# A gated decoder layer on one core: row sums turned on TensorE, and two tiles of h turned by DMA

## The chip, the cores and the metric

The kernel runs on one core of a Trainium2 chip. The metric is the device time of one execution in microseconds (us), taken as the median of repeated runs. A core has five instruction streams that run side by side and meet at semaphores: TensorE (PE in the profile, with PEld for its weight loads), VectorE (DVE), ScalarE (ACT), GpSimd (POOL) and SyncE (SP, which here only issues DMAs). Matrix products read from the on-chip memory SBUF and write to the accumulation memory PSUM; DMAs move data between SBUF and the device memory. Most DMAs are issued from SP's queue, a few from POOL's.

## The reference

One layer works on 1024 prompt tokens and 8 sample tokens, with a model width of 1024, all in 32-bit floats. What matters here:

```python
xn = _rmsnorm(h, pre_g)
proj = jnp.einsum('bld,de->ble', xn, w_in)          # 1024 -> 7 x 1024
u, v, z_a, x_b, z_b, g_a, g_b = jnp.split(proj, SPLITS, axis=-1)
vn = _layernorm(jax.nn.gelu(v), ln_g, ln_b)
y_a = u * _chunk_spatial_mix(vn, w_s, b_s) * jax.nn.silu(z_a)
...
m = (jax.nn.sigmoid(g_a) * jnp.einsum('ble,ed->bld', y_a, w_pa)
     + jax.nn.sigmoid(g_b) * jnp.einsum('ble,ed->bld', y_b, w_pb))
h = h + _rmsnorm(jnp.einsum('bld,de->ble', m, w_out), post_g)
e = jnp.einsum('blp,pd->bld', p, w_ple)
gate = jax.nn.sigmoid(jnp.einsum('bld,de->ble', _rmsnorm(h, ple_in_g), w_pg))
h = h + _rmsnorm(gate * e, ple_out_g)
```

Two places bear on the change. The spatial mix multiplies each chunk of 128 tokens by a lower-triangular 128x128 matrix per head, tril(W_s), and adds a bias b_s. Since vn = (v normalised) * ln_g + ln_b, the part with ln_b is the row sum of tril(W_s) times ln_b, one number per head and token. And the last product, with w_pg, needs h with the features along the partitions, while h is made with the tokens along them; so h has to be transposed.

## The kernel before

All large products are done with one level of Strassen's scheme (seven products P1 to P7 for a 2x2 block product) on operands that are split into a high and a low part, each product in three matmuls of reduced-precision format. A step of the stream is one such product: 12 matmuls of 512 columns, or 24 of 260. The stream runs over v, g_a, (u, z_a), (x_b, z_b and the pooling), g_b, w_pa, w_pb, then w_out and at last w_pg ("the gate product"), the last two by pairs of token tiles: pair i holds the tiles 2i and 2i+1 of 128 tokens each.

The order of instructions is not written out by hand beyond the opening. Every operation is handed to a planner (lines 56 to 300), which notes a due time for it, from its place in TensorE's stream and what depends on it, then plays all engines through with a duration for each kind of operation, and emits the instructions of each engine in the order that comes out. Work that is due later gives way to work that is due earlier; an instruction that has begun is not interrupted, and each engine runs its list in order. The first three steps are in a fixed order; from line 1733 on, the planner orders all of it. Tiles in SBUF come from a pool of 46 slots (line 31), and a slot is given to the next user when its last reader is done. The weights of a step are split three steps ahead (line 32).

The row sums. `ln_loads` (line 931) loads W_s as the tile ws and ln_g, ln_b as 16 rows of the tile lnvec. `spatial_weights` (line 943), put after the first step of g_a (line 1267), clears the upper triangles, sums the rows on VectorE into a tile of 128 tokens x 8 heads (rowsums), and stores it to device memory by a DMA that turns it on the way, so that the destination has 8 rows of 128. It also transposes the eight matrices on TensorE (bank psw) and lnvec into columns (bank lncol). `spatial_offsets` (line 963), eight steps later, reads the rows back, broadcast to all partitions (tile off), and makes of them the offsets that the users of z_a add.

The turning of h. For each tile t, `out_finish` (line 1405) scales h, adds the layer's input to it by an accumulating DMA from POOL's queue, and stores the result. `gate_norm` (line 1421) takes the sum of squares on ScalarE for the normalisation. `gate_input` (line 1438) transposes h in eight 128x128 blocks on TensorE into two PSUM banks (pht), which ScalarE copies into big, the operand of the gate product. They are hung on the steps of the following pair (lines 1564 to 1566): `out_finish` after its first step, `gate_norm` after its second, `gate_input` after its seventh. Tiles of h are handled in the order 1, 0, 3, 2 and so on; the gate product reads pair 0 first, and its splits of big are written to tiles named hw.

There is another way in the code already, under `if t in BY_DMA`, and the tuple BY_DMA (line 1416) is empty. It is the way that v is turned in `v_planes` and `v_join` (lines 866 and 875): ScalarE copies the upper and the lower 16-bit halves of the 32-bit words into two planes (for h in a new slot, also named hw), one transposing DMA on SP's queue turns both planes at once, and ScalarE joins the halves into big in two instructions.

Of the kernel before, what the change touches and what calls it, by code (L numbers as in the profile page):

```python
# [15 lines left out]
P = 128  # L16
D = 1024
NB = D // P
# [282 lines left out]
@with_exitstack  # L301
def tile_hybrid_step(ctx, tc, *args):
    hybrid_step(ctx, tc, *args)


def hybrid_step(
# [7 lines left out]
    nc = tc.nc  # L314
# [15 lines left out]
    def slot(name, shape=(P, T), dt=F32):  # L330
        n_name[0] += 1
        return plan.tile(spool.tile(list(shape), dt, tag="slot", name=f"{name}_{n_name[0]}", bufs=SLOTS,
                                    padded_shape=None), "slot")
# [5 lines left out]
    def bank(name):  # L339
        n_name[0] += 1  # L340
        return plan.tile(bankp.tile([P, 512], F32, tag="bank", name=f"{name}_{n_name[0]}"), "bank")
# [8 lines left out]
    def split(src, hi, lo):  # L350

        nc.scalar.activation(out=hi, in_=src, func=AF.Copy)
        nc.vector.tensor_tensor(out=lo, in0=src, in1=f32(hi), op=ALU.subtract)

    def dma(out, in_, by=None):
        (by or nc.sync).dma_start(out=out, in_=in_)
# [11 lines left out]
    ident = cpool.tile([P, P], F32, tag="ident", name="ident")  # L368
# [3 lines left out]
    nc = plan  # L372
# [16 lines left out]
    def root(part, n=P, r=None):  # L389

        t, r = sm("ms"), sm("rstd") if r is None else r
        nc.vector.tensor_scalar(out=t[:n], in0=part[:n], scalar1=EPS, scalar2=None, op0=ALU.add)
        nc.gpsimd.tensor_tensor(out=r[:n], in0=t[:n], in1=mhalf[:n], op=ALU.pow)
        return r
# [144 lines left out]
    class Features:  # L539

        new = staticmethod(lambda: region("acc"))
        sums = (P, 2, WIDE)
# [15 lines left out]
    class Tokens:  # L558
# [4 lines left out]
        sums = (P, 2, HALF)  # L563
# [359 lines left out]
    lnt = {}  # L923
# [7 lines left out]
    def ln_loads():  # L931
        lnt["ws"] = slot("ws", (P, NB, P))
        dma(lnt["ws"], w_s.rearrange("h t s -> t h s"))
        vec = lnt["vec"] = slot("lnvec", (P, P))
        for i, v in enumerate((ln_g, ln_b)):
            dma(vec[i * NB : (i + 1) * NB, :], v[0].rearrange("(k p) -> k p", p=P))

    def ln_rows():
        lnt["g"] = row_broadcast(ln_g[0], "lng")
# [3 lines left out]
    def spatial_weights():  # L943

        ws = lnt["ws"]
        nc.gpsimd.affine_select(out=ws, in_=ws, pattern=[[0, NB], [-1, P]], compare_op=ALU.is_ge,
                                fill=0.0, base=0, channel_multiplier=1)
        sums = cpool.tile([P, NB], F32, tag="rowsums", name="rowsums")
        nc.vector.tensor_reduce(out=sums, in_=ws, op=ALU.add, axis=mybir.AxisListType.X)
        dma(kept["rowsum"].rearrange("h t -> t h"), sums)  # L950
        lnt["wst"] = []
        for h4 in range(0, NB, 4):
            w = slot("wst", (P, 4, 2, P), F32R)
            ps = bank("psw")
            for i in range(4):
                nc.tensor.transpose(ps[:, i * P : (i + 1) * P], ws[:, h4 + i, :], ident)
            split(ps.rearrange("p (h t) -> p h t", t=P), w[:, :, 0], w[:, :, 1])
            lnt["wst"].append(w)
        ps = bank("lncol")
        nc.tensor.transpose(ps[:, : 2 * NB], lnt["vec"][: 2 * NB, :], ident[: 2 * NB, : 2 * NB])  # L960
        nc.vector.tensor_copy(lncol, ps[:, : 2 * NB].rearrange("p (i k) -> p i k", i=2))

    def spatial_offsets():

        off = lnt["off"] = slot("off", (P, NB, P))
        dma(off, kept["rowsum"].partition_broadcast(P))
        for h in range(NB):
            nc.vector.scalar_tensor_tensor(out=off[:, h], in0=off[:, h], scalar=lncol[:, 1, h : h + 1],
                                           in1=lnt["bs"][:, h * P : (h + 1) * P], op0=ALU.mult, op1=ALU.add)
# [31 lines left out]
    kept = {}  # L1001
# [262 lines left out]


    at(vsteps[2][3], ln_loads)
    at(gasteps[0][0], spatial_weights)
    for i, u in enumerate(vusers):

# [54 lines left out]
    p, l, c = gbsteps[2], gbsteps[3], pasteps[0]  # L1324
    turn_over(yaop, l, [*l[1:], c[0]])
    p, l, c = pasteps[2], pasteps[3], pbsteps[0]
# [86 lines left out]

    rin = lambda t: vsums[: rows(t), t, :1]

    BY_DMA = ()

    def words_of(t):
        return big.bitcast(U16)[:, :, 2 * t * P : 2 * (t + 1) * P]

    def gate_norm(t):
# [6 lines left out]
        root(n, r, rin(t))  # L1428
        if t not in BY_DMA:
            return  # L1430
# [7 lines left out]
    def gate_input(t):  # L1438
# [5 lines left out]
        for k4 in (slice(0, 4), slice(4, NB)):  # L1444
            if t in BY_DMA:
                nc.scalar.activation(out=words_of(t)[:, k4].rearrange("p k (t w) -> p k t w", w=2),
# [323 lines left out]
```

## Time and profile before

| what | value |
|---|---|
| median of three runs | 993.81 us (993.17 to 995.39) |
| the profiled execution | 993.5 us |
| its span, first to last instruction | 991.8 us |
| mean granted clock of TensorE | 0.998 |
| instructions | 15979 |
| moved by DMAs | 173.48 MB in 106154 packets, of which 25503 under 512 bytes |

In lines of the profile, an entry such as `big<-pht` names the tile that is written and the one that is read, without buffer numbers. L299 is a helper through which all planned operations pass, so tiles and engines, not lines, tell the operations apart. In the timeline the columns are start, length, engine, line, operation, `out<-in`, shapes and a count where several were merged; brackets give the idle time of the engine before it and what ended it. Lengths of matmuls contain their pipeline, so what one costs is seen from the starts of its neighbours. SPq and POOLq are the issuing of DMAs on those queues; the length is that of the issue, not of the transfer.

### The profile page before, as it was taken

The page shows a single profiled execution, that of the slowest core. Times are in us where ns is not written, and L with a number is a line of the kernel's source. Part 1 is how long each engine was busy: PE and PEld are TensorE (multiplying, and loading weights), DVE is VectorE, ACT ScalarE, POOL GpSimd, SP SyncE. Part 2 cuts the span into 40 slices and gives each one's busy share as a digit, 9 for nine tenths or more (in the row PEclk, how much of TensorE's full clock was granted, in tenths as well). Part 3 has the DMA queues.
Part 4 walks back from the last instruction along what each step waited for, and adds up shares of the span by engine and source line. Part 5 has one row for each costly group of instructions (what it writes and reads, how often), then busy time and mean ns, then how long its engine had stood idle before and what let it go on. Part 6 is the DMA issues. An engine that isn't in the chain of part 4 may idle for free. (4 is left out here: it accounts for less than half of the span.)

```text
span 991.8 us, 15979 instructions
## 1 busy us (share of the span) xinstructions
PE 977.3 (99%) x6102; PEld 877.1 (88%) x6102; DVE 797.6 (80%) x1238; ACT 523.4 (53%) x884; POOL 68.5 (7%) x142
## 2 busy tenths in 40 slices
PE   8999999999999999999999999999999999999996
PEld 7789989999998999999999999999999988888885
DVE  6796569787769888979897987697799898779596
ACT  7778987565434433344442333552353364677463
POOL 2100001000000000000000100000000001213111
PEclk9999999999999999999999999999999999999999
DMA  9335573322373353656735085973663543399546
GB/s 338 132 104 117 119 151 128 128 84 78 118 259 145 120 204 135 224 197 212 259 119 193 15 272 203 318 285 121 241 229 137 176 176 69 84 308 362 137 109 191
DMA packets 106154, 173.48 MB, mean 175 GB/s; under 512 B 25503, under 2 KB 64879, under 8 KB 106070
## 3 DMA queue, kind: packets, MB, share of 16 engines
q1 hardware_dynamic: 103982, 165.08, 49.0%
q0 software_dynamic: 2048, 7.37, 4.4%
q8 instruction: 48, 0.79, 0.3%
q14 instruction: 28, 0.23, 0.1%
q10 hardware_dynamic: 48, 0.01, 0.0%
HBM read 114.84 MB, written 53.87 MB: 170 GB/s over the span
## 5 line engine op out<-in xcount | busy, mean ns | idle before, releaser
L299 DVE TENSOR_TENSOR u<-acc,u 128x520 f32<-128x520 f32 (+1 forms) x90 | 62.7, 696 | 38.3 <-PE acc L299 35.0
L299 POOL TENSOR_TENSOR rstd<-ms,mhalf 128x1 f32<-128x1 f32 (+1 forms) x36 | 30.4, 848 | 192.5 <-DVE ms L299 191.5
L299 POOL MEMSET u<- 128x8 f32 x35 | 4.5, 164 | 502.6 <-PE acc L299 251.3
L299 ACT ACTIVATE u<-acc 128x512 f32<-128x512 f32 x39 | 23.3, 597 | 25.0 <-PE acc L299 24.6
L299 ACT ACTIVATE paw<-pas 128x512 fp32r<-128x512 f32 x16 | 10.1, 628 | 30.5 <-DVE pas L299 25.2
L299 ACT ACTIVATE pbw<-pbs 128x512 fp32r<-128x512 f32 x16 | 10.0, 629 | 28.0 <-DVE pbs L299 24.9
L299 DVE TENSOR_TENSOR big<-big 128x1024 f32<-128x1024 f32 (+4 forms) x20 | 23.6, 1219 | 0.0
L299 ACT ACTIVATE big<-mix 128x256 f32<-128x256 f32 x32 | 12.1, 383 | 18.1 <-PE mix L299 17.3
L299 ACT ACTIVATE big<-v 128x1024 uint16<-128x1024 uint16 x16 | 18.5, 1175 | 5.1 <-DMA v<-vw 5.1
L299 PE MATMUL accm<-qh,wpoolw 128*128 128x260 f32 (+1 forms) x96 | 20.9, 319 | 0.0
L299 ACT ACT_TABLE_LOAD x13 | 16.7, 1283 | 7.2 <-PE acc L299 6.3
L299 ACT ACTIVATE zbw<-zbs 128x512 fp32r<-128x512 f32 x16 | 10.1, 629 | 16.6 <-DVE zbs L299 11.6
L299 DVE TENSOR_TENSOR acc<-acc,u 128x512 f32<-128x512 f32 (+1 forms) x16 | 11.2, 701 | 8.7 <-PE acc L299 8.7
L299 DVE TENSOR_TENSOR v<-acc,u 128x520 f32<-128x520 f32 (+1 forms) x9 | 6.3, 697 | 14.3 <-PE acc L299 14.2
L299 ACT ACTIVATE gbw<-gbs 128x512 fp32r<-128x512 f32 x16 | 10.0, 626 | 14.6 <-DVE gbs L299 12.1
L299 ACT ACTIVATE zaw<-zas 128x512 fp32r<-128x512 f32 x16 | 10.0, 629 | 14.5 <-DVE zas L299 9.1
L299 PEld LDWEIGHTS accm<-qh,wpoolw 128*128 128x128 f32 x96 | 15.6, 188 | 1.9
L299 ACT ACTIVATE gb<-gb 128x1032 f32<-128x1032 f32 (+1 forms) x8 | 6.8, 855 | 19.3 <-DVE gb L299 19.3
L299 ACT ACTIVATE uw<-us 128x512 fp32r<-128x512 f32 x16 | 10.0, 626 | 13.2 <-DVE us L299 11.2
L299 ACT ACTIVATE vw<-v 128x1024 uint16<-128x1024 uint16 x16 | 16.1, 1045 | 0.5 <-DVE v L299 0.5
L299 DVE TENSOR_TENSOR big<-mix,big 128x256 f32<-128x256 f32 x32 | 12.7, 421 | 4.6 <-ACT big L299 4.1
L299 ACT ACTIVATE junk<-ge 128x512 bf16<-128x512 f32 (+2 forms) x19 | 11.5, 608 | 7.5 <-DVE ge L299 7.1
(686 smaller groups left out, 3624.2 us busy)
## 6 DMA issues: line engine op xcount, KB each, us to landing
ga<-ga SPq DMA_DIRECT2D x16, 516.0 KB
gb<-gb SPq DMA_DIRECT2D x16, 516.0 KB
ya<-za SPq DMA_DIRECT2D x8, 516.0 KB
yb<-zb SPq DMA_DIRECT2D x8, 516.0 KB
x<-in_x_prompt_dram SPq DMA_DIRECT2D x8, 512.0 KB
vraw<-in_w_in_dram SPq DMA_DIRECT2D x8, 512.0 KB
e<-e SPq DMA_DIRECT2D x8, 512.0 KB
garaw<-in_w_in_dram SPq DMA_DIRECT2D x8, 512.0 KB
```

Of the source, the lines that this page charges most:

```text
L299: getattr(getattr(self.nc, e), method)(*args, **kwargs)
```

## The change

Two edits. The row sums are turned by a TensorE transpose into the bank that lncol already uses, copied by VectorE into a second half of the tile lnvec, and stored as eight rows of 128 floats. And BY_DMA becomes (0, 1): the tiles 0 and 1 of h take the other way. The words_of, gate_norm and gate_input functions themselves are unchanged.

```diff
     def ln_loads():
...
-        vec = lnt["vec"] = slot("lnvec", (P, P))
+        vec = lnt["vec"] = slot("lnvec", (P, 2 * P))
         for i, v in enumerate((ln_g, ln_b)):
-            dma(vec[i * NB : (i + 1) * NB, :], v[0].rearrange("(k p) -> k p", p=P))
+            dma(vec[i * NB : (i + 1) * NB, :P], v[0].rearrange("(k p) -> k p", p=P))
...
     def spatial_weights():
...
         nc.vector.tensor_reduce(out=sums, in_=ws, op=ALU.add, axis=mybir.AxisListType.X)
-        dma(kept["rowsum"].rearrange("h t -> t h"), sums)
...
         ps = bank("lncol")
-        nc.tensor.transpose(ps[:, : 2 * NB], lnt["vec"][: 2 * NB, :], ident[: 2 * NB, : 2 * NB])
+        nc.tensor.transpose(ps[:, : 2 * NB], lnt["vec"][: 2 * NB, :P], ident[: 2 * NB, : 2 * NB])
+        nc.tensor.transpose(ps[:NB, P : 2 * P], sums, ident)
         nc.vector.tensor_copy(lncol, ps[:, : 2 * NB].rearrange("p (i k) -> p i k", i=2))
+        turned = lnt["vec"][:NB, P:]
+        nc.vector.tensor_copy(turned, ps[:NB, P : 2 * P])
+        dma(kept["rowsum"], turned)
...
-    BY_DMA = ()
+    BY_DMA = (0, 1)
```

## The prediction

> **What bounds the kernel now.** The page comes first, for the share of each engine, and then the waits of TensorE and the table by stretches.
>
> ```profile
> PE 977.3 (99%) x6102; PEld 877.1 (88%) x6102; DVE 797.6 (80%) x1238; ACT 523.4 (53%) x884; POOL 68.5 (7%) x142
> ```
>
> TensorE (PE) is busy for 977.3 of 991.8 us. The page's chain that ended last does not help here: it covers only the last 5 us. So I ask which waits PE has at all.
>
> ```profile
> PE warm L299 <- POOL ident masks.py:199: 1.9, 1, 1.9
> PE e L299 <- ACT big L299: 1.4, 1, 1.4
> PE acc L299 <- DVE u L299: 0.9, 1, 0.9
> PE acc L299 <- ACT gaw L299: 0.7, 1, 0.7
> PE pst L299 <- DVE ms L299: 0.6, 1, 0.6
> PE pht L299 <- ACT big L299: 0.3, 1, 0.3
> PE acc L299 <- DVE vw L299: 0.2, 1, 0.2
> PE state L299 <- DVE big L299: 0.2, 1, 0.2
> ```
>
> Columns: total, times, longest. All of them together are 6.2 us in eight places. The stretches show the same around the tiles that the change touches:
>
> ```profile
> 25.00:127.00 102.00, 100.43 (x631) 89.33 (x630) 72.03 (x101) 81.91 (x145) 4.99 (x10) 1.00 0.41 114
> ...
> 838.00:848.00 10.00, 10.00 (x45) 8.10 (x44) 6.33 (x13) 6.09 (x13) 2.02 (x3) 1.00 0.48 148
> 848.00:858.00 10.00, 10.00 (x53) 8.36 (x52) 7.80 (x14) 8.28 (x18) 3.66 (x6) 1.00 0.16 21
> ...
> 984.00:992.00 8.00, 0.00 (x0) 0.00 (x0) 3.91 (x9) 1.40 (x5) 0.59 (x1) 0.68 0.42 160
> ```
>
> After the length come the busy times of PE, PEld, DVE, ACT and POOL, then the granted clock (1.00), the DMA share and GB/s. From 838 to 858 PE never idles. It ends by 984, and a tail of about 8 us follows that PE has no part in. So the time is a sum of PE's instructions plus a head and a tail: what is taken off PE's list comes off the time one for one, as long as the engines that replace it keep out of PE's way. That is the whole question for this change.
>
> **The change, part two: two tiles of h.** First what leaves PE.
>
> ```profile
> L299 PE MATMUL pht<-ident,h x64: 270/272/328, 848.3 to 920.4; 128*128 128x128 f32 x64
> L299 ACT ACTIVATE big<-pht x16: 577/590/607, 850.6 to 920.9; 128x512 f32<-128x512 f32 x16
> ...
> 848.02 0.39 PE L299 MATMUL acct<-woT1h,mw 128*128 128x512 f32 x1
> 848.25 1.04 PE L299 MATMUL pht<-ident,h 128*128 128x128 f32 x8
> 849.04 0.48 PE L299 MATMUL acct<-woB11h,mw 128*128 128x512 f32 x1
> 849.36 0.39 PE L299 MATMUL acct<-woB11l,mw 128*128 128x512 f32 x1
> ...
> 854.67 1.03 PE L299 MATMUL pht<-ident,h 128*128 128x128 f32 x8
> ```
>
> Eight tiles have eight transposes each. The 272 ns of one is its length in a pipeline and no price. The price is read from the starts: the matmul at 848.02 is followed after its usual 0.23 us by the first transpose, at 848.25; the second matmul behind the eight starts at 849.36. Of these 1.11 us one matmul's 0.23 would be there anyway, so a tile costs PE 0.88 us (0.11 a transpose). The two groups, at 848.25 and 854.67, are tiles 1 and 0: **1.76 us leave PE**, with four evictions from PSUM on ACT of 0.59 us, 2.36 us.
>
> What comes instead runs already, for v, on tiles of the same size:
>
> ```profile
> L299 ACT ACTIVATE vw<-v x16: 1040/1042/1059, 72.9 to 133.2; 128x1024 uint16<-128x1024 uint16 x16
> L299 ACT ACTIVATE big<-v x16: 1160/1174/1196, 79.4 to 147.9; 128x1024 uint16<-128x1024 uint16 x16
> ...
> 74.94 1.93 SPq L299 DMA_TRANSPOSE v<-vw  x1
> ...
> 79.35 1.19 ACT L299 ACTIVATE big<-v 128x1024 uint16<-128x1024 uint16 x1 [1.19 <-DMA v<-vw]
> ```
>
> For each tile ACT makes two planes (1.04 us each) and, later, two joins (1.17 us each), and SP issues one transposing DMA. For two tiles ACT gains 4 x 1.04 + 4 x 1.17 = 8.84 us and loses 2.36, net 6.5. The first transposing DMA was issued at 74.94 and what waited for it ran at 79.35, so 4.4 us from issue to use. Does ACT have room?
>
> ```profile
> 841.78 1.06 ACT L299 ACTIVATE big<-h 128x1024 f32<-128x1024 f32 x1 [2.44 <-DMA h<-in_x_prompt_dram]
> ...
> 849.33 0.63 ACT L299 ACTIVATE junk<-h 128x512 bf16<-128x512 f32 x1 [2.60 <-DVE h L299]
> ...
> 861.37 0.60 ACT L299 ACTIVATE junk<-acct 128x512 bf16<-128x512 f32 x1 [3.60 <-PE acct L299]
> ...
> 880.78 0.62 ACT L299 ACTIVATE hw<-big 128x512 fp32r<-128x512 f32 x1
> ```
>
> The brackets are ACT's idle time ahead of the instruction. Between the first tile's squares and 861.37 it has holes of 2.44, 2.60 and 3.60 us, 8.6 in all, against 6.5 net. The first hole, which waits for tile 0's h, is as long as the two planes of tile 1 (2.08). The first reader of the turned tiles is the split at 880.78, so the joins may also run later than 861. I cost ACT's 6.5 us at nothing; without that cover the part that reaches PE is a stall (rival D).
>
> Now the queues. The transposing DMA writes h in place, so it must wait for the planes and until h's own store to memory has been read out, and SP stands still meanwhile.
>
> ```profile
> 838.22 4.02 SPq L299 DMA_DIRECT2D h<-h  x2
> 852.01 0.28 SPq L299 DMA_DIRECT2D h<-hs  x1
> 860.94 7.20 SPq L299 DMA_DIRECT2D h<-h  x2
> 868.25 3.46 SPq L299 DMA_DIRECT2D wgB<-wgleft  x2
> ...
> h<-in_x_prompt_dram POOLq DMA_DIRECT2D x8, 512.0 KB, 7.8
> ```
>
> From 838 to 868 SP issues nothing but five stores of h, which the code reads back only once the gate product is under way; the loads for the next product begin at 868.25. How long such a store takes is not shown; I bound it below by nothing and above by the 7.8 us of the same tile's accumulating load. Late case: the second store of the first row goes out by 842.24, ends by 850.0, the transposing DMA takes 4.4, and four joins end by about 859: 21 us ahead of 880.78. No one waits behind SP. POOL's queue gets nothing. The two extra plane tiles hold two of the kernel's 46 slots for some 10 us; the trace does not show free slots, and I take nothing, with rival D's stall as the other end.
>
> On this the Trainium skill speaks against the change: "VectorE: DVE Perf Modes", section "The three transpose paths", gives 390 ns to TensorE and 1309 ns to a DMA for a 128x128 block of 2-byte elements, and its rules prefer TensorE where PSUM will do. A tile here is 16 such blocks, so by that figure an estimate of 20.9 us for one DMA if the blocks follow each other; the trace has 4.4 us, and by the measurement the sum stands.
>
> **The change, part one: the row sums.**
>
> ```profile
> 127.86 0.38 SPq L299 DMA_DIRECT2D rowsum<-rowsums  x1
> 133.32 6.74 SPq L299 DMA_TRANSPOSE v<-vw  x2
> 160.47 1.42 SPq L299 DMA_DIRECT2D off<-rowsum  x1
> ...
> 126.61 1.22 DVE L299 TENSOR_REDUCE rowsums<-ws 128x8 f32<-128x1024 f32 x1
> 134.29 0.17 DVE L299 COPY lncol<-lncol 128x16 f32<-128x16 f32 x1
> ...
> 133.51 0.23 PE L299 MATMUL lncol<-ident,lnvec 16*128 16x16 f32 x1
> ...
> 140.80 2.25 ACT L299 ACTIVATE big<-v 128x1024 uint16<-128x1024 uint16 x2 [2.62 <-DMA v<-vw]
> ```
>
> The store at 127.86 writes 1024 single words of 4 bytes; it becomes eight rows of 512 bytes, issued after the copy, near 135. Its reader comes at 160.47, so neither its old nor its new duration is on any path. Added on PE is one transpose beside that of lncol: between the 0.11 of a transpose in a row and the 0.23 of a full matmul, both worked out above. I take 0.11, the price of the same operation. It needs the reduction, which ends at 127.83, 5.7 us ahead of PE's place, so no wait. On DVE comes one small copy, near the 0.17 of lncol's. SP's two transposing DMAs of v stand at 133.32; the new store may be put between them and hold the second up until the copy is done, some tenths of a us. The other way, these two took 6.74 us to issue, where the one at 74.94 took 1.93, and ACT then waited 2.62 us for them: if the 1024 words ahead of them were in their way, that wait shrinks. I take nothing for either; rival B has the gain.
>
> **Sum.** -1.76 + 0.11 = -1.65 us, all of it PE's. The profiled execution took 993.5 us (span 991.8 and 1.7 around it), so 991.85; it lies 0.3 below the median of the three runs, 993.81, so the forecast for the median is **992.2 us** (-0.17%). About 0.2%, 2.0 us, is what a measurement of this kernel can tell from no change, so this most likely counts as the same.
>
> **Rivals.** The instructions' order is planned anew from the row sums on, since the planner replays all with changed costs; that is what can differ beyond the sum.
>
> A, the forecast, 992.2 with its own range 991.6 to 992.8: chance 0.45. For it: PE's full stretches, and ACT's and SP's holes.
>
> B, more is gained, chance 0.27. PE's 0.7 us on gaw lies behind ACT's wait for the DMA at 140.80; with it gone and, in the new order, the 0.3 on pht too, -1.65 - 1.0 = -2.65: 991.2. Against it: no row shows that the words slowed the transposing DMAs.
>
> C, given back, chance 0.16: the new order leaves PE with new waits. Those of the list that are not at the start are 0.2 to 1.4 us each; one of 1.4 gives -0.25, 993.6. Here too belongs, with a hundredth, that it does not do what it says, so that pht keeps 64 transposes: 993.8.
>
> D, slower, chance 0.09: ACT becomes the bound between 838 and 862. Its instructions are not interrupted, so a plane or a join of over 1 us stands in front of a weight split (mw) or an eviction that PE needs. If all 6.5 net reach PE, +6.5 - 1.65 = +4.9, 998.7; it decides from 3.65 us, over half of them, where the loss passes 2.0. Against it: in 25 to 127 ACT is busy 81.9 of 102 us with such planes and joins, and PE loses 1.6 us there in all.
>
> E, the transposing DMA lands late and ACT stands at a join, chance 0.03. PE's weights are split three steps ahead, a step being about 2.8 us (849.04 to 854.67 holds two), 8.4 in all; for a loss over 2.0 the landing must be late by 8.4 + 3.65 = 12.1 us, so take 16.5 instead of 4.4. At 7.5, from 133.32 to 140.80, the trace's longest, PE sees nothing. With two behind each other at 7.5 the second is 10.6 late and PE stalls 2.2: 994.4. By the Trainium skill's figure above, the estimate of 20.9 us would stall PE by 8.1.
>
> **How the numbers follow.** Faster by over 0.2% is below 991.8: nearly all of B (0.25) and the lower part of A (0.11), 0.36. Slower by over 0.2% is above 995.8: D and E, 0.12. The rest, 0.52, is the same. The range leaves out the last of B below 990.7 and D with the worst of E above 994.6.
>
> **What would show it.** Right: pht has 48 transposes and 12 evictions; PE's busy time falls by some 1.6; PE has still no wait from 838 to 862; the four joins run before 870. B: the issue of v's transposing DMAs near 133 is shorter and the wait on gaw gone. C: new rows in the list of PE's waits. D: PE waits for ACT mw or acct there. E: an ACT wait for a DMA into h over 8 us. Wrong outright would be a change in the tail after the last matmul (about 8 us), which the sum leaves alone.

## The result and the profile after

The changed kernel takes 991.5 us (991.0 to 992.33, 10 runs), the kernel before on the same chip 994.29 us (992.72 to 995.99, 10 runs): a ratio of 0.9972 (95% interval 0.9963 to 0.9982), 2.8 us less. The profiled execution took 991.0 us, its span is 989.3 us; before it was 993.5 and 991.8.

The page of the changed kernel, and its groups of instructions that write or read pht (columns of a group: count, then shortest, median and longest ns, first and last start):

```profile
PE 975.0 (99%) x6087; PEld 875.3 (88%) x6087; DVE 797.4 (81%) x1239; ACT 529.6 (54%) x888; POOL 69.9 (7%) x142
```

```profile
L299 PE MATMUL pht<-ident,h x48: 270/272/327, 867.4 to 917.5; 128*128 128x128 f32 x48
L299 ACT ACTIVATE big<-pht x12: 575/593/607, 868.1 to 918.1; 128x512 f32<-128x512 f32 x12
```

Sixteen transposes and four evictions are gone, ACT's busy time has grown by 6.2 us, and PE's has fallen by 2.3, not by 1.65. To see where, three instructions serve as milestones, which both kernels have. From the timeline of PE, of the kernel before (its lncol, at 133.51, stands in the prediction):

```profile
832.51 0.39 PE L299 MATMUL sps<-woB11h,mst 128*128 128x512 f32 x1
...
983.38 0.28 PE L299 MATMUL acct<-wgB21h,hw 128*128 128x256 f32 x1
```

and of the kernel after, with the new transpose and the one behind it:

```profile
133.37 0.23 PE L299 MATMUL lncol<-ident,lnvec 16*128 16x16 f32 x1
133.53 0.27 PE L299 MATMUL lncol<-ident,rowsums 128*8 128x128 f32 x1
133.64 0.38 PE L299 MATMUL vt<-ident,v 128*8 128x128 f32 x2
...
831.44 0.39 PE L299 MATMUL sps<-woB11h,mst 128*128 128x512 f32 x1
...
980.54 0.28 PE L299 MATMUL acct<-wgB21h,hw 128*128 128x256 f32 x1
```

The last stretch holds the tiles of h: 983.38 - 832.51 = 150.87 us before, 980.54 - 831.44 = 149.10 after, **1.77 less**. The middle stretch, from lncol to sps, holds what the row sums do: 699.00 before, 698.07 after, **0.93 less** where 0.11 more was forecast. And the tail from PE's last matmul to the end of the span is 8.42 before and 8.76 after, 0.34 more, which is why the span lost 2.5 and PE's last matmul 2.84. The other 0.14 came ahead of lncol, whose start lies between 132.82 and 133.68 in the runs below.

For the last stretch, the timelines of SP and then of ACT, and the windows, of the kernel after (DMA_TRANSPOSE is the transposing DMA of a tile, uint16 the joins):

```profile
845.52 2.24 SPq L299 DMA_TRANSPOSE h<-hw  x1
...
852.72 5.21 SPq L299 DMA_TRANSPOSE h<-hw  x1
```

```profile
854.33 2.25 ACT L299 ACTIVATE big<-h 128x1024 uint16<-128x1024 uint16 x2
...
861.22 1.17 ACT L299 ACTIVATE big<-h 128x1024 uint16<-128x1024 uint16 x1
...
862.92 1.18 ACT L299 ACTIVATE big<-h 128x1024 uint16<-128x1024 uint16 x1
```

```profile
838.00:848.00 10.00, 10.00 (x45) 8.09 (x44) 7.81 (x13) 9.12 (x18) 2.94 (x3) 1.00 0.57 165
848.00:858.00 10.00, 10.00 (x45) 8.16 (x44) 6.68 (x12) 8.55 (x14) 3.53 (x5) 1.00 0.66 116
```

PE is busy for all 20 us and no join has a bracket: ACT never stood waiting for a transposing DMA of h. The 6.09 us of ACT in the first window became 9.12; the holes were used.

For the middle stretch, the waits of PE, of the kernel after:

```profile
PE acc L299 <- DVE u L299: 0.5, 1, 0.5
PE pht L299 <- ACT big L299: 0.3, 1, 0.3
...
PE acc L299 <- DVE ga L299: 0.2, 1, 0.2
```

The 0.7 on gaw has gone, 0.2 on ga has come in its place, and the 0.9 on u (near 320, far from both edits) is 0.5 in this execution and 0.8 in a second one of the same kernel. In the other runs below it lies between 0.7 and 1.4, with the words or without, so the 0.4 that it gives here is chance. The reason for the first change is in the timeline of the kernel after:

```profile
133.17 5.21 SPq L299 DMA_TRANSPOSE v<-vw  x2
...
138.29 1.19 ACT L299 ACTIVATE big<-v 128x1024 uint16<-128x1024 uint16 x1 [1.28 <-DMA v<-vw]
...
139.61 0.64 SPq L299 DMA_DIRECT2D rowsum<-lnvec  x1
```

The pair of transposing DMAs of v is issued in 5.21 us in place of 6.74, ACT waits 1.28 us for it in place of 2.62, and the new store comes behind the pair. That is what the prediction named as the sign of rival B. So the open question is whether the 1024 single words were in the pair's way, or whether the new order of the instructions around it made the difference.

### The profile page after: what moved, and what is told of

It is laid out like the page before. It is cut to its first block, busy times and chain, and to the rows that moved or that the text cites. A ratio compares the mean times of both kernels' runs of the same rounds, so it can differ in the third digit from the quotient of the medians.

```text
span 989.3 us, 15945 instructions
## 1 busy us (share of the span) xinstructions
PE 975.0 (99%) x6087; PEld 875.3 (88%) x6087; DVE 797.4 (81%) x1239; ACT 529.6 (54%) x888; POOL 69.9 (7%) x142
## 5 line engine op out<-in xcount | busy, mean ns | idle before, releaser
L299 PE MATMUL accm<-qh,wpoolw 128*128 128x260 f32 (+1 forms) x96 | 20.9, 319 | 0.0
L299 ACT ACTIVATE big<-h 128x1024 f32<-128x1024 f32 (+1 forms) x12 | 13.0, 1092 | 5.0 <-DMA h<-in_x_prompt_dram 5.0
```

Of the source, the lines that this page charges most:

```text
L299: getattr(getattr(self.nc, e), method)(*args, **kwargs)
```

## The experiments

Two theories stand at the start. The first: the words hold up the pair behind them, and each edit brings its own part. The rival: the words do nothing, and the new plan moved a wait. The middle stretch (lncol to sps) and the last one (sps to the last matmul) were read as above; they are given in us. Each ratio is to executions of the kernel before in the same set; their median lay between 994.11 and 995.4, so times of different sets can differ by over a us by themselves. Two runs that change the tiles' way follow behind the table's.

| run | words stored | us (lowest to highest) | ratio to before | middle | last |
|---|---|---|---|---|---|
| before | ahead of the pair | 994.29 (992.72-995.99) | 1 | 699.00 | 150.87 |
| after | not | 991.5 (991.0-992.33) | 0.9972 (0.9963-0.9982) | 698.07 | 149.10 |
| after, again | not | 991.69 (991.14-993.28) | 0.9969 (0.9960-0.9979) | 698.36 | 149.10 |
| row sums alone | not | 992.85 (992.44-994.22) | 0.9978 (0.9968-0.9987) | 698.77 | 150.83 |
| tiles alone | ahead of the pair | 993.07 (991.84-994.85) | 0.9981 (0.9970-0.9993) | 699.64 | 149.08 |
| words kept | ahead of the pair | 995.56 (992.8-996.63) | 1.0001 (0.9991-1.0012) | 703.52 | 149.10 |
| words early | 10 us earlier | 991.37 (991.01-991.72) | 0.9971 (0.9958-0.9984) | 698.59 | 149.07 |
| words twice | ahead of the pair, two stores | 1010.33 (1009.08-1011.6) | 1.0159 (1.0142-1.0176) | 716.37 | 149.10 |
| words moved | ahead of two loads and the pair | 1002.11 (1001.26-1002.33) | 1.0068 (1.0052-1.0084) | 709.19 | 149.08 |
| words late | behind the pair and two loads | 999.3 (998.67-1004.29) | 1.0048 (1.0031-1.0065) | 706.75 | 149.14 |
| a load ahead of v's pair | not | 992.46 (991.9-992.89) | 0.9972 (0.9962-0.9981) | 699.61 | 149.04 |
| an accumulating DMA there | not | 995.81 (994.31-998.69) | 1.0013 (0.9997-1.0028) | 703.78 | 149.09 |

In these runs the last column takes one of two values, whatever else was done: about 150.85 with eight tiles turned on PE, 149.04 to 149.14 with six. The middle column is where the cases differ.

### Each edit alone

The changed kernel with `BY_DMA = ()`:

> Only the row sums change; BY_DMA is empty, so pht has its 64 transposes again. Up to the out product the order of instructions is that of the changed kernel. Theory 'two separate gains' (the tiles are worth PE's 1.76 us, and the row sums the other 1.1 us of the profiled difference): about 1.0 us faster than before, 993.2, with the list of PE's waits as in the changed kernel (no 0.7 on gaw, 0.5 in place of 0.9 on u). Theory 'the row sums cost their transpose' (my sum): 0.1 us slower than before, 994.4.

The changed kernel with the row sums as before:

> Only BY_DMA = (0, 1); the row sums are stored as words as before. Theory 'two separate gains': 1.75 us faster than before, 992.5, with the waits on gaw (0.7) and u (0.9) still there, and no PE wait between 838 and 862. Theory 'the tiles bring all of it': as the changed kernel, 991.5. Rival D (ACT becomes the bound): no gain at all, 994.3.

And the changed kernel a second time, in a later set:

> The changed kernel itself, as the yardstick for this set: 991.5. If the two parts add up (the row sums alone took 2.4 us off, the tiles alone 2.2), it is 4.6 us faster than the kernel before in the same set; by the first comparison only 2.8.

Each edit alone is faster than before, by 0.22% and by 0.19%; both together by 0.28 to 0.31%. In its own set the changed kernel is 2.9 us faster than before, not the 4.6 that the two parts would add up to. The interval of each part reaches about half its size to either side, so whether they add up isn't settled by the times; the stretches say 1.77 for the tiles. With the tiles alone, the timelines of SP and ACT still show the slow pair:

```profile
132.91 7.67 SPq L299 DMA_TRANSPOSE v<-vw  x2
...
141.16 1.19 ACT L299 ACTIVATE big<-v 128x1024 uint16<-128x1024 uint16 x1 [3.40 <-DMA v<-vw]
```

PE waits 1.6 us for gaw there. With the row sums alone the pair takes 4.72 us, and there is no wait on gaw.

### The words, with nothing else moved

In the changed kernel, the old store as well, behind the transposes of W_s. The instructions of the other engines are the same and in the same order, and the eight rows are stored besides. This kernel does one unneeded store.

```diff
+        dma(kept["rowsum"].rearrange("h t -> t h"), sums)
         ps = bank("lncol")
```

> The changed kernel, and besides its rows the old store of 1024 single words, in the old place in SP's queue, right ahead of the two transposing DMAs of v near 133. All other instructions of all engines are in the order of the changed kernel. Theory 'words in the way': the two transposing DMAs take 6.5 us or more to issue again in place of 5.2, ACT waits for them 2 to 3 us in place of 1.3, PE waits again near 150, and 0.3 to 0.7 us are lost: 991.9 to 992.2. Theory 'new order': the issue may be slower, but the time stays at 991.5 within 0.2, with no new PE wait.

The stall came, and cost far more than the 0.3 to 0.7 us expected: it takes back all that both edits gave, 1.0001 (0.9991 to 1.0012). In the timeline of ACT, and in the windows of the run:

```profile
141.67 1.17 ACT L299 ACTIVATE big<-v 128x1024 uint16<-128x1024 uint16 x1 [5.20 <-DMA v<-vw]
```

```profile
134.00:136.00 2.00, 2.00 (x10) 1.63 (x9) 1.18 (x5) 2.00 (x6) 0.07 (x1) 1.00 1.55 198
136.00:140.00 4.00, 4.00 (x31) 3.78 (x30) 2.84 (x4) 0.47 (x3) 0.47 (x1) 1.00 1.57 28
```

The pair is issued in 8.58 us; it starts at 198 GB/s and falls to 28 from 136 to 140, where the changed kernel has 193. PE waits 2.9 us for ACT behind it. As the order is the changed kernel's, the rival (a new plan alone) falls: the words make the stall. What a stall costs PE is another matter: 0.7 and 1.6 us of waiting in the old order (before, tiles alone), 2.9 and a spell at a lower clock in the new one. With one trace of each, what the order and what chance has in that isn't separated. Then the same store right behind the reduction, which the changed kernel does 12 us earlier than the one before:

```diff
         nc.vector.tensor_reduce(out=sums, in_=ws, op=ALU.add, axis=mybir.AxisListType.X)
+        dma(kept["rowsum"].rearrange("h t -> t h"), sums)
```

> The changed kernel and the store of 1024 words besides, as in the run with the words kept, but issued right after the reduction, near 117, behind the pair of v's transposing DMAs at 113 and 16 us ahead of the next pair at 133; the rest in the changed kernel's order. Theory 'words in the way' in the form that they must be in flight with a transposing DMA: they are over by 133, the pair there takes 5 us to issue and the time is the changed kernel's within 0.3. In the form that any word store costs its DMA engines' time wherever it stands: 993.5 or more, as near 133.

Same words, same packets, no loss. The windows of that run (columns as in the prediction: the last is GB/s, the one ahead of it the DMA share):

```profile
127.00:130.00 3.00, 3.00 (x29) 3.00 (x27) 0.11 (x1) 1.68 (x10) 0.00 (x0) 1.00 0.09 12
130.00:133.00 3.00, 3.00 (x27) 2.87 (x25) 1.87 (x3) 3.00 (x5) 0.00 (x0) 1.00 0.95 266
```

The words were issued at 117.30. The two loads behind them, lng and lnb, were issued at 125.57 and 126.17, but move only from 130 on; in the changed kernel the window from 127 to 130 has 302 GB/s. So the words still held something up 10 us later; no one needed those loads yet. Next, two stores of words near 127 (the second into memory that is overwritten later; both unneeded):

```diff
+        dma(kept["rowsum"].rearrange("h t -> t h"), sums)
+        dma(kept["ya"][:NB, :P].rearrange("h t -> t h"), sums)
         ps = bank("lncol")
```

> As the run with the words kept near 133, but two such stores, 2048 words. If the loss is the words' own time ahead of the transposing DMAs, the pair's issue grows again by what one store added (3.4 us: 5.2 to 8.6), to about 12, and PE's wait by as much, so 3 us slower than with one store, about 998. If one store already costs all there is (the DMA merely loses its place), no further change: 995.5.

Far more than twice the loss, 18.8 us beside the changed kernel where one store cost about 4. The pair was issued over 20.88 us from 133.03; in the timeline of ACT and the waits of PE:

```profile
154.49 1.17 ACT L299 ACTIVATE big<-v 128x1024 uint16<-128x1024 uint16 x1 [17.61 <-DMA v<-vw]
```

```profile
PE acc L299 <- ACT ga L299: 15.3, 1, 15.3
```

### How long, and what is held up

An attempt to move the words about 10 us ahead, behind the pair of 113, in the kernel with the tiles alone, with the row sums in a function of their own:

```diff
+    def row_sums():
...
+        dma(kept["rowsum"].rearrange("h t -> t h"), sums)
...
+    at(vsteps[3][5], row_sums)
```

> Tiles 0 and 1 by DMA, and no turning of the row sums on TensorE: they are stored as 1024 words as in the kernel before, only that the reduction and the store are done some ten us earlier, right behind v's pair of transposing DMAs at 113. If what the row sums' edit brings is only that the words are out of the way of the pair at 133: as fast as the changed kernel, 991.4 within 0.3, the pair at 133 takes about 5 us to issue and PE has no wait on gaw or ga over 0.3. If turning them on TensorE and storing rows matters by itself: between the tiles alone (993.1) and the changed kernel, the pair as slow as there.

The edit missed its aim: the planner left the words at 127.95 and put the loads lng (128.42) and lnb (129.07) behind them. But it shows the words by themselves. First its windows; then, from its DMA view, the packets from 128 to 130, from 132 to 136 and from 136 to 140:

```profile
130.00:133.00 3.00, 3.00 (x28) 3.00 (x27) 1.96 (x3) 2.59 (x4) 0.00 (x0) 1.00 0.15 10
133.00:136.00 3.00, 3.00 (x18) 2.47 (x17) 1.83 (x6) 3.00 (x6) 0.00 (x0) 1.00 0.21 15
136.00:139.00 3.00, 3.00 (x23) 2.82 (x23) 0.94 (x2) 2.25 (x4) 0.54 (x1) 1.00 0.20 12
139.00:142.00 3.00, 3.00 (x18) 2.56 (x17) 0.00 (x0) 0.00 (x0) 0.00 (x0) 1.00 0.67 175
```

```profile
DMA packets 1040, 0.00 MB, mean 2 GB/s; under 512 B 1040, under 2 KB 1040, under 8 KB 1040
...
DMA packets 18, 0.07 MB, mean 18 GB/s; under 512 B 0, under 2 KB 0, under 8 KB 18
...
DMA packets 14, 0.06 MB, mean 14 GB/s; under 512 B 0, under 2 KB 0, under 8 KB 14
```

All 1040 small packets have passed by 130, within 2 us. It is the time behind them that is lost: for 9 us, to about 139, two loads of 512 KB trickle at 10 to 15 GB/s, a few packets a us, though only a fifth of the DMA engines' time is busy. Then the rate recovers. The pair, issued at 133.41, follows, and ACT waits 10.84 us for it.

If this is a dead time of the DMA engines behind the words, it should strike whatever is under way, not only what is issued after them. The last run on this has the words behind the pair and two loads of weights (garaw), at the place of the eight rows; a DVE instruction of eight elements per partition ties them to it:

```diff
-        dma(kept["rowsum"], turned)
+        late = cpool.tile([P, NB], F32, tag="late", name="late")
+        nc.vector.scalar_tensor_tensor(out=late, in0=lncol[:, 0], scalar=0.0, in1=sums, op0=ALU.mult, op1=ALU.add)
+        dma(kept["rowsum"].rearrange("h t -> t h"), late)
```

> The changed kernel, with the row sums stored by the old DMA of 1024 single words, but issued where the changed kernel issues its eight rows: behind v's last two transposing DMAs and two weight loads, near 139. (An extra DVE instruction of 8 elements a partition ties it to that place; TensorE's transpose stays, its result is not used.) If the words cost time only by holding up the transposing DMAs issued behind them on the same queue: the pair's issue takes 5 to 6 us, ACT waits under 2 us for it, no wait of TensorE on ga or gaw over 0.5, and 991.4 us, a ratio near 0.997 to the kernel before. If the words themselves cost (by their packets, wherever they stand), or hold up the weight load issued near 152: 993.5 to 994.5, ratio 0.999 to 1.000.

Both expectations failed, and in the direction of the dead time: 999.3 us, worse than the words ahead of the pair. The pair was fine (4.94 us). The timelines of SP and DVE, then the packets from 142 to 144 and from 146 to 151:

```profile
138.15 1.07 SPq L299 DMA_DIRECT2D garaw<-in_w_in_dram  x2
139.27 0.50 SPq L299 DMA_DIRECT2D rowsum<-late  x1
...
151.32 0.69 DVE L299 TENSOR_TENSOR gas<-garaw,garaw 128x512 f32<-128x512 f32 x1 [6.32 <-DMA garaw<-in_w_in_dram]
```

```profile
DMA packets 1430, 0.64 MB, mean 322 GB/s; under 512 B 991, under 2 KB 1368, under 8 KB 1430
...
DMA packets 48, 0.12 MB, mean 24 GB/s; under 512 B 19, under 2 KB 19, under 8 KB 48
```

The second garaw was issued **ahead** of the words, and still landed at 151.3, where in the changed kernel DVE used it at 145.99. The words pass between 142 and 144, and the 48 packets of the next 5 us, which in the changed kernel had gone by then (one packet in the same 5 us), take until 151. PE stands 6.8 us for DVE's ga. So the words need not be ahead of a transfer in the queue to hold it up; it is enough that it isn't finished when they pass.

Is it the words, or any transfer near the pair? One plain load of 512 KB ahead of the pair, into a slot nobody reads:

```diff
+            for i in range(1 if (pair, m) == (NPAIR - 1, 0) else 0):
+                beside = slot("beside", (P, D))
+                nc.vector.tensor_copy(beside.bitcast(U16)[:, :2], words[:, 0, :2])
+                dma(beside, x_prompt[i * P : (i + 1) * P, :])
             nc.sync.dma_start_transpose(out=v.rearrange("p (k c) -> p k c", c=P),
```

> The changed kernel with one unneeded plain load of 512 KB issued right ahead of v's pair of transposing DMAs at 133, where no accumulating DMA is in flight. Theory 'only single words are poison': the load costs its own 1.5 to 3 us of the DMA engines at most, the pair takes 5 to 8 us to issue, ACT waits at most 4 us, and the time is within 2 us of the changed kernel. Theory 'any DMA in flight ahead slows the pair, by far more than its own time': the pair takes 10 us or more, PE waits 5 us or more, 996 or more.

128 times the bytes of the words, and by the ratios no loss beside the two runs of the changed kernel (0.9972 against 0.9972 and 0.9969); by the medians, of different sets, 0.8 to 1.0 us. The pair takes 6.78 us and PE waits 1.1 us for gaw; the plan also orders some instructions behind the pair anew. It is not traffic as such.

### What the tiles' way can cost

Four tiles in place of two (`BY_DMA = (0, 1, 2, 3)`):

> The changed kernel with BY_DMA = (0, 1, 2, 3): the two tiles of pair 1 go by DMA too. If a tile is worth its 0.88 us of PE and ACT and SP have room: 1.76 us faster than the changed kernel, 989.7, pht at 32 transposes. Rival D or E: ACT's further 6.5 us stand among the cuts of the gate product's operands, which start near 876, and SP's transposing DMAs among their loads; then PE waits of 1 to 4 us appear after 876 and the time is 990.7 to 994.

1013.59 us, a ratio of 1.0178 (1.0139 to 1.0218), far over both expectations. The DMAs of the tiles 2 and 3 fall where the loads of the next product, and the accumulating loads from POOL's queue, also run. Timeline of SP, windows and PE's waits of that run:

```profile
874.48 23.43 SPq L299 DMA_TRANSPOSE h<-hw  x2
```

```profile
880.00:888.00 8.00, 7.50 (x33) 5.78 (x31) 1.37 (x3) 2.57 (x4) 0.87 (x1) 1.00 1.39 66
...
893.00:900.00 7.00, 1.94 (x8) 1.57 (x8) 1.08 (x1) 2.33 (x3) 0.00 (x0) 0.50 1.27 75
```

```profile
PE pht L299 <- DMA h<-in_x_prompt_dram: 8.9, 1, 8.9
```

The two DMAs were issued over 23.43 us; the DMA share is over 1, yet only 66 to 75 GB/s move, and PE stands 8.9 us for the pht of a later tile, whose accumulating load of h comes late among them. Here rival E's kind of loss came, at another place. To bring it about at the forecast's place, two plain loads were put ahead of each of the two tiles' DMAs (unneeded loads into slots nobody reads):

```diff
+        for i in range(2):
+            beside = slot("beside", (P, D))
+            nc.vector.tensor_copy(beside.bitcast(U16)[:, :2], words[:, 1, :2])
+            dma(beside, x_prompt[(2 * t + i) * P : (2 * t + i + 1) * P, :])
         h_of[t] = h.bitcast(U16).rearrange("p (k t) -> p k t", t=P)
```

> The changed kernel with two unneeded loads of 512 KB issued right ahead of each of the two transposing DMAs of h, so that they are in flight together. This asks why with four tiles a pair of transposing DMAs took 24 us. Theory 'plain loads in flight slow a transposing DMA': from its issue to the joins 10 us or more in place of about 5 to 8, with the DMA engines busy and few GB/s. Theory 'it was the accumulating DMAs of POOL': the loads cost their own 3 us or so each (1 MB at some 340 GB/s), the joins come at most 5 us later, and the time is within 0.5 of the changed kernel.

997.81 us, 1.0043 (1.0026 to 1.0059). The first DMA, at 846.15, was joined at 850.97, 4.8 us later, without a wait; the second, from the timelines of SP and ACT, after 13.8 us:

```profile
856.87 6.10 SPq L299 DMA_TRANSPOSE h<-hw  x1
...
870.71 2.24 ACT L299 ACTIVATE big<-h 128x1024 uint16<-128x1024 uint16 x2 [5.22 <-DMA h<-hw]
```

Both had loads ahead; the second also had accumulating loads of POOL's queue beside it (854.31 and 859.18). So, ahead of v's pair, one accumulating DMA of 512 KB into a cleared slot:

```diff
+                nc.gpsimd.memset(beside, 0.0)
+                nc.gpsimd.dma_start(out=beside, in_=x_prompt[i * P : (i + 1) * P, :], accum_op=ALU.add)
             nc.sync.dma_start_transpose(out=v.rearrange("p (k c) -> p k c", c=P),
```

> The changed kernel, with one more accumulating DMA of 512 KB on POOL's queue, into a cleared slot that nobody reads, put by the planner beside v's last pair of transposing DMAs near 133. It asks whether what slowed h's second transposing DMA with loads beside it (13.8 us) was the accumulating DMAs of POOL's queue that ran then too. If accumulating DMAs are what slows a transposing one: the pair's issue takes over 10 us, ACT waits over 6 us, and 995 to 998 us. If an accumulating DMA is no worse than a plain load (pair 6.8 us, ACT's wait 2.5, 992.5 us in that run): 992 to 993.5 us, pair 5 to 8 us.

It falls between the two expectations: 995.81 us, but the pair was issued in 6.39 us and ACT waited 3.6 and 2.0 us for its halves, not over 6. This run lost 4.1 to 4.3 us beside the changed kernel, more than the one with the plain load. But not all of it is the DMA's: PE waited 2.3 us for DVE's sv, and the plan of this run has ACT's step for sv behind the first join (140.13) where the changed kernel has it ahead (134.97). So what an accumulating DMA costs by itself isn't shown. What makes transposing DMAs beside loads as slow as in the two runs before stays open.

## Why the prediction was right, and where it was wrong

The time, 991.5, lies in the range, 0.7 below the forecast of 992.2 and nearest to rival B's 991.2.

- **The two tiles: right, in place and size.** Forecast -1.76; the last stretch has -1.77, and again in each run with the tiles (149.04 to 149.14 against 150.83 and 150.87). The price of 0.11 a transpose, from the starts of its neighbours and not from the 270 ns of its length, holds.
- **The transpose of the row sums: right.** From its start to the next is 0.11 (133.53 to 133.64).
- **ACT's holes: right.** +6.2 us against 6.5, no wait of PE from 838 to 858, last join at 862.92, first reader of the turned tiles at 877.97. Rival D did not come. The estimate of 20.9 us worked out from the Trainium skill's figure (the page "VectorE: DVE Perf Modes", section "The three transpose paths") isn't borne out: a tile of h was turned and joined 4.8 us after the issue in the run with loads beside, although two loads were issued ahead of it. In the four-tile run two DMAs took over 23 us, but beside other transfers.
- **"Neither its old nor its new duration is on any path": the step that failed.** The store of 1024 words was cleared by its reader, 33 us later. But its path goes through the transfers beside it: it stalls them, ACT stands at the join of v, and PE at gaw. The prediction saw the sign (6.74 us of issue against 1.93) and took nothing for it, as no row showed the words to be the cause.
- **Such rows were there.** The windows of the kernel before and of the kernel after, from 133 to 139:

```profile
133.00:136.00 3.00, 3.00 (x18) 2.43 (x18) 1.82 (x6) 3.00 (x6) 0.00 (x0) 1.00 0.65 44
136.00:139.00 3.00, 3.00 (x24) 2.86 (x23) 2.00 (x3) 2.15 (x4) 0.54 (x1) 1.00 1.29 128
```

```profile
133.00:136.00 3.00, 3.00 (x18) 2.40 (x17) 2.00 (x7) 3.00 (x6) 0.00 (x0) 1.00 0.62 114
136.00:139.00 3.00, 3.00 (x24) 2.86 (x23) 2.06 (x3) 1.72 (x7) 0.54 (x1) 1.00 1.17 204
```

  At nearly the same share of busy DMA engines, the pair moved at 44 and 128 GB/s before, at 114 and 204 after. A high share with a low rate, right behind a store in single words, was to be seen before the change.
- **Rival B: its mechanism, and its price in part by luck.** The wait on gaw went, as it said; 0.2 on ga came, and pht kept its 0.3; of rival C's new waits there is none beyond that 0.2 in the middle and the last stretch. The middle stretch gained 0.93. Of this the waits named give 0.7 - 0.2 + 0.4 (u) - 0.11 = 0.8. The 0.4 of u is chance, so the row sums' own part in these two executions is some 0.4 us, not B's 1.0; with the row sums alone, whose u was 1.2, the stretch gained 0.23. Against the tiles alone, where gaw cost 1.6, the same edit saves 1.4 us of waiting.
- **The tail: wrong by 0.34 us.** The prediction left it alone and called a change in it the sign of being wrong outright; it grew by 0.34 us. The last instruction of DVE, in the kernel before and after:

```profile
987.38 1.42 DVE L299 SCALAR_TENSOR_TENSOR ge<-ge,rstd,hback 128x512 f32<-128x512 f32 x2 [0.44 <-POOL rstd L299]
```

```profile
984.55 1.41 DVE L299 SCALAR_TENSOR_TENSOR ge<-ge,rstd,hback 128x512 f32<-128x512 f32 x2 [0.44 <-POOL rstd L299]
```

  From PE's last matmul to the end of this is 5.42 us in both, so the engines' part is unchanged. What follows, with the last store, takes 3.0 us before and 3.3 after. It goes with the tiles: the whole tail is 8.42 and 8.35 us in the two runs with eight tiles on PE, 8.66 to 8.80 in all others but the one with loads beside (8.48). So some 0.3 of the tiles' 1.77 us is given back here; why is open.
- **The spread.** The words' price isn't constant: with them ahead of the pair the middle stretch was 699.00, 699.64 and 703.52, without them 698.07 to 698.77. That fits the wider spread of the kernel before. Of its 87 executions beside the experiments, the 23 with a mean granted clock of 0.996 or less took 995.18 us or more, and the 28 with 0.998 or more took 995.03 or less; all 22 executions of the changed kernel had 0.997 or 0.998. So in some executions of the kernel before the stall may well last long enough for the clock to fall, as in words kept. That is not shown: the profiled one, at 993.5 and with a wait of 0.7, is not of these, and no trace here is of such an execution. It would explain why the row sums alone give 2.2 us by the ratio and so little by the stretches.

## What to carry to other kernels

A transfer is not free because its reader is late: look at what else is on the DMA engines in the 10 us after it, and at GB/s beside the DMA share. A store in single words is worth turning on an engine first, even on the engine that bounds the kernel, where 0.11 us of it saved 0.5 to 1.4 us of waiting in the traces, and some 2 us by the ratio of the row sums alone; or it goes where nothing else moves. And count a gain on the bounding engine from start to start between milestones that both kernels have: the last stretch gave the tiles' part to within 0.1 us in ten runs, which the medians could not. Then take out the waits that vary from run to run, like that on u, before the rest is called a gain.

## What the runs showed of the hardware

- **A dead time behind a store of single words.** 1024 words of 4 bytes pass as packets in about 2 us. After that plain loads move at 10 to 15 GB/s for some 9 us (words moved) and at 24 for 5 us (words late), where loads otherwise reach over 250; in words early the stall lasts until 10 us behind the words. Transposing DMAs fare unevenly: in words kept the pair moved at 198 GB/s for 2 us before it fell to 28. Two stores were dead for longer (1 GB/s from 131 to 139, 34 to 145, 58 to 151). The cause inside the chip stays open, and no run separates the size of the words from their order in memory, where each of the 128 partitions writes eight words 512 bytes apart. The Trainium skill, "DMA: Bandwidth & Descriptors", section "Specifications", says that transfers below 512 bytes make the DMA engine read, modify and write, and gives no time for it. No run here shows that this is what happens; and size below 512 alone is not enough, since the packets of the transposing DMAs are also below it and move at over 200 GB/s. The page "VectorE: DVE Perf Modes", section "The three transpose paths", of the same skill warns that a plain DMA which transposes by its strides is far slower than a transposing one. The runs agree, though for transfers of very different size: the 4 KB of words move at 2 GB/s in words moved, and the pair of transposing DMAs at over 200 in the changed kernel. They add that others pay for it.
- **A short wait of PE can cost more than itself.** The wait of 1.6 us in tiles alone left the granted clock at 1.00. After one of 2.3 us, with an accumulating DMA beside v's pair, the windows of that run have:

```profile
148.00:151.00 3.00, 3.00 (x18) 2.98 (x18) 2.93 (x8) 2.99 (x6) 0.00 (x0) 0.50 0.08 11
151.00:154.00 3.00, 3.00 (x16) 3.00 (x15) 0.82 (x4) 2.50 (x4) 0.00 (x0) 0.50 0.00 0
```

  PE works on for 6 us at half the clock, some 3 us more than it would need. So the words late, with a wait of 6.8 us, lost 8.7 in the middle stretch. But the length of the wait alone doesn't decide. In the run with loads beside the tiles' DMAs PE waited 2.8 us, until 874.86, and the clock stayed at 1.00:

```profile
872.00:876.00 4.00, 1.16 (x6) 0.97 (x6) 1.45 (x3) 4.00 (x9) 0.55 (x1) 1.00 0.80 223
```

  No run here tests what decides. The Trainium skill, "TensorE: Matmul & The Clock Gate", section "Part 1: The HAM clock gate (the "warmup" mystery)", has the clock halved after an idle window of about 3.4 us; the halving agrees, but here a wait of 2.3 us was enough in one run, and one of 2.8 us was not in another.
